# A hybrid decoder layer: the state space model on quarter-array products, its taps turned by transposes, and attention scores with the masks first

## The chip, the cores and the metric

The kernel runs on one core of a Trainium2 chip. The metric is the device time of one execution in microseconds. Before the change three runs took 1202.39, 1202.74 and 1205.45 us; the median is 1202.74 us. All durations below come from one profiled execution of the kernel before, which itself took 1202.62 us.

## The reference

One decoder layer for two groups of requests that share weights: a prompt (16 learned meta tokens and 256 positions) and 8 sample sequences with one position each. D_MODEL is 2048; the first 1024 channels of the projection drive a state space model (SSM) of 64 groups with 16 channels and one 64-dimensional complex diagonal state each, and 16 query heads on 4 key-value heads do sliding-window attention.

```python
u, q, k, v = project(rmsnorm(x))                 # one matrix product with w_in
# state space model, per group g (16 channels h, 64 states p):
x_t  = coef * (b @ u_t);  s_t = a * s_{t-1} + x_t            # complex, diagonal
y_t  = Re(c @ s_t) + d_skip * u_t
y    = gelu(y);  y = y * sigmoid(y @ w_glu + b_glu)
# attention, banded in blocks of 128, with a learned sink per head:
o    = softmax([mask + scale * q k^T | sink])[..., :-1] @ v
x    = x + [rmsnorm(y) | rmsnorm(o)] @ w_out
x    = x + ConvFFN(rmsnorm(x))                   # 2048 -> 2 * 5632 -> 2048
```

Outputs are the layer's result, new caches of keys and values, and the new SSM and convolution states.

## The kernel before

The activations are kept transposed: channels on the 128 partitions, 280 positions (266 after the norm of the SSM and attention results) along the free axis. Every large product streams its weights once: a 512 KB tile `w` comes by DMA from the sync engine (SP) into one of three buffers, ScalarE (ACT) casts it to `wh`, VectorE (DVE) subtracts that to get the low part `wl`, and TensorE (PE) does three products for each pair of tiles (`mm3`, L233 to L235). A helper records every elementwise operation of two inputs at line L72, so these are known by their tile names.

PE runs its instructions in the order in which the code is written; the order of the other engines comes from a scheduler when the kernel is built. Each engine works through its own queue in order. The stages that matter:

- Attention and the projection of `u` (104.78 to 216.91 us). Eight groups, four of kind "A" (144 keys: the meta tokens and one block) and four of kind "B" (256 keys), go through `att_group` (L831) in turn; between its steps stand the PE instructions of the projection that makes `u`. A group has three PE steps. Scores: four heads, each with one product of the identity `identb` with the mask (L840) and one of 64 rows of `qT` with `kd` (L841), all added in one tile `sps`. Then the softmax on DVE and ACT (L856, L862) leaves `P`; eight transposes make `ppt` (L870); four products with the values make `ops` (L879), its two halves of the partitions one after the other.
- The SSM stage (216.91 to 334.47 us). The sequence is cut into chunks of CH = 4 positions, so 76 columns (68 chunks and 8 samples) stand for all positions. Iteration i of eight handles 8 of the 64 groups as 4 pairs r. `ssm_load` brings `u` and fills block-padded copies of the maps (`Bb`, `C0b`, `DI`) for it; `ssm_in` transposes `Bb` into `Li`; `ssm_fir` makes the products of the first taps (`kps`, L1077) and copies them into `FIR`; `ssm_state` takes the chunk inputs (`vps`, L1095), then runs a chain of ten DVE instructions: rotate (`z`, `q`), two scans, rotate back into `S`; `ssm_out` makes the output (`yps`, L1136) from `S` with the map `Cb`, filled by `ssm_maps`, and from `U` with `FIR`.
- The same stage carries the attention half of the output projection (`oa`): blocks of 12 matmuls (`acc<-ah`), and a table OA says how many stand at three places of each iteration. It is not changed.
- The gated product with `w_glu`, the SSM half of `w_out`, and the feed-forward network (to the end).

In the loop (L1176 on) the order written for PE within iteration i is: the inputs of state i+1 (`vps`), `oa` blocks, the output of i (`yps`), `oa` blocks, the transposes of i+2 (`lps`), `oa` blocks, the taps of i+2 (`kps`).

Of the kernel before, what the change touches and what calls it, by code (L numbers as in the profile page):

```python
# [22 lines left out]
NS = 8  # L23
# [4 lines left out]
CH = 4  # L28
# [13 lines left out]
def rope_tables():  # L42
# [12 lines left out]
        "vec1": dict(lam_re=32, lam_im=32, log_dt=32, ssm_d=32),  # L55
# [10 lines left out]
def body(ctx, tc, I, O, dbg=None):  # L66
# [389 lines left out]
    def prm_maps():  # L456
# [38 lines left out]
        R0, N0 = CC[:, :, 0, 0, :], CC[:, :, 1, 0, :]  # L495
        A.copy(R0, vsl("c_re").rearrange("p (r h) -> p r h", h=16))
        A.activation(N0, vsl("c_im").rearrange("p (r h) -> p r h", h=16), AF.Copy, scale=-1.0)
        yield
        for h in range(0, 32, 8):
            r_ = slice(h, h + 8)  # L500
            pr, pi = (PW[:, k, r_, :, None].to_broadcast([128, 8, 4, 16]) for k in range(2))
            Rb, Nb = (z[:, r_, None, :].to_broadcast([128, 8, 4, 16]) for z in (R0, N0))
            mul(w1, Rb, pr)
            yield
            mul(w2, Nb, pi)
            yield
            add(CC[:, r_, 0, 1:, :], w1, w2)
            yield
            mul(w1, Nb, pr)
            yield  # L510
            mul(w2, Rb, pi)
            yield
            sub(CC[:, r_, 1, 1:, :], w1, w2)
            yield
# [83 lines left out]
    sdp = sp.tile([128, 32], F32, name="sdp")  # L598
# [14 lines left out]
    ud = dram.tile([8, 128, CH, UC], F32, name="ud")  # L613
    yd = dram.tile([8, 128, 4, SC_], F32, name="yd")
# [175 lines left out]
    CC = sp2.tile([128, 32, 2, CH + 1, 16], F32, name="CC")  # L790
# [40 lines left out]
    def att_group(nm, kv):  # L831
# [45 lines left out]
        for par in range(2):  # L877
            for bi, (c, n, vv) in enumerate(blocks):
# [153 lines left out]
    Bbs = [sw.tile([128, 4, 2 * CH, 2, 16], F32, name=f"Bb{i}", bufs=1) for i in range(2)]  # L1032
    C0s = [sw.tile([128, 4, 2, 2, 16], F32, name=f"C0b{i}", bufs=1) for i in range(2)]
    Cb = sw.tile([128, 4, 2 * CH, 2, 16], F32, name="Cb", bufs=1)
    FIRs = [sw.tile([128, 4, CH, 32], F32, name=f"FIR{i}", bufs=1) for i in range(2)]
    DIs = [sw.tile([128, 4, 32], F32, name=f"DI{i}", bufs=1) for i in range(2)]
    for t in (Bbs[0], C0s[0]):
        V.memset(t, 0.0)
    for t in (DIs[0], FIRs[0], Bbs[1], C0s[1], Cb, DIs[1], FIRs[1]):
        G.memset(t, 0.0)  # L1040
    SO4 = SO.rearrange("p c b r -> p c r b")
    Li, U2, S, d0 = {}, {}, {}, {}

    def ssm_load(i):

        r4 = slice(4 * i, 4 * i + 4)
        U2[i] = sw.tile([128, 4, UC], F32, name="U2", bufs=3)
        for j in range(CH):
            nc.sync.dma_start(U2[i][32 * j:32 * j + 32], ud[i, :, j, :].rearrange("(r q) c -> q r c", r=4))
# [4 lines left out]
        mul(DIs[i % 2][96:128], sdp[96:128, r4, None].to_broadcast([32, 4, 32]),  # L1054
            ident[96:128, None, 96:128].to_broadcast([32, 4, 32]), eng=G)
# [3 lines left out]
    def bv(i):  # L1059
        return Bbs[i % 2].rearrange("p r (c j) g h -> p r c (j g h)", c=2)  # L1060

    def ssm_in(i):
        Li[i] = sw.tile([128, 4, 2, 128], F32, name="Li")
        lps = big.tile([128, 4, 2, 128], F32, name="lps", tag="big")
        for r in range(4):
            for c in range(2):
                PE.transpose(lps[:, r, c, :], bv(i)[:, r, c], ident)  # L1067
        for h in range(2):
            A.copy(Li[i][:, 2 * h:2 * h + 2], lps[:, 2 * h:2 * h + 2])

    def ssm_fir(i):
        FIR = FIRs[i % 2]
        C0v = C0s[i % 2].rearrange("p r c g h -> p r c (g h)")
        kps = one.tile([128, 4, 32], F32, name="kps", tag="one")
        for r in range(4):
            for c in range(2):
                PE.matmul(kps[:, r, :], bv(i)[:, r, c], C0v[:, r, c], start=c == 0, stop=c == 1)  # L1077
        add(kps[96:128], kps[96:128], DIs[i % 2][96:128])
        A.copy(FIR[:, :, 3], kps)
        for j in range(3):  # L1080
            A.copy(FIR[32 * j:32 * j + 32, :, 2], kps[32 * j + 32:32 * j + 64])
        A.copy(FIR[0:64, :, 1], kps[64:128])
        A.copy(FIR[0:32, :, 0], kps[96:128])

    def ssm_state(i):
# [6 lines left out]
        vps = big.tile([128, 4, 2, 128], F32, name="vps", tag="big")  # L1092
        for r in range(4):
            for c in range(2):
                PE.matmul(vps[:, r, c, :SC_], Li[i][:, r, c, :], U2[i][:, r, NS:UC], start=True, stop=True)  # L1095
# [3 lines left out]
        def both(x):  # L1099
            return x[:, :, None].to_broadcast([128, 4, 2, SC_])  # L1100

        mul(z.rearrange("p c r n -> p r c n"), vps[:, :, :, :SC_], both(cs))
        mul(q.rearrange("p c r n -> p r c n"), vps[:, :, ::-1, :SC_], both(sn))
# [17 lines left out]
    def ssm_maps(i):  # L1121
        r4 = slice(4 * i, 4 * i + 4)
        for g in range(2):
            p = slice(64 * g, 64 * g + 64)
            A.copy(Cb[p, :, :, g, :].rearrange("p r (c j) h -> p r c j h", c=2), CC[p, r4, :, 1:, :])

    def ssm_out(i):
        Cv = Cb.rearrange("p r (c j) g h -> p r c (j g h)", c=2)
        yps = one.tile([128, 4, SC_], F32, name="yps", tag="one")
        for r in range(4):  # L1130
            for part in range(3):
                if part < 2:
                    lhs, rhs = Cv[:, r, part], S[i][:, part, r, 0:SC_]
                else:
                    lhs, rhs = FIRs[i % 2][:, r].rearrange("p j q -> p (j q)"), U2[i][:, r, 0:SC_]
                PE.matmul(yps[:, r, :], lhs, rhs, start=part == 0, stop=part == 2)  # L1136
        ysb = sw.tile([128, 4, SC_], F32, name="ysb")
        A.copy(ysb, yps)
# [9 lines left out]
    def gelu(i):  # L1148
        yr = gy.tile([128, CH, SC_], F32, name="yr", bufs=2)
        for r in range(4):  # L1150
            nc.sync.dma_start(yr[32 * r:32 * r + 32], yd[i, :, r, :].rearrange("(j q) c -> q j c", j=CH))
# [214 lines left out]
def prepare(I):  # L1366
# [9 lines left out]
    def gp(v):  # L1376
        v = v.reshape((32, 128) + v.shape[2:])
        return np.moveaxis(v, 0, 1).reshape(128, -1)

    qg, kg = I["q_norm_g"][0], I["k_norm_g"][0]  # L1380
# [3 lines left out]
    v = dict(norm_mix_g=col(I["norm_mix_g"]), norm_ffn_g=col(I["norm_ffn_g"]), ssm_out_g=col(I["ssm_out_g"]),  # L1384
             attn_out_g=col(I["attn_out_g"]), b_glu=col(I["b_glu"]),
# [5 lines left out]
             h0=np.concatenate(h0, 1), ssm_d=np.tile(I["ssm_d"][0].reshape(32, 32).T, (4, 1)),  # L1391
# [40 lines left out]
```

## Time and profile before

| what | value |
|---|---|
| median of three runs | 1202.74 us |
| profiled execution, its own time | 1202.62 us (span in the trace 1200.4 us) |
| PE busy, share of the span | 1172.8 us, 98% |
| chain that ended last: PE, DVE, ACT | 91%, 3%, 3% of the span |
| DVE busy, share of the span | 813.0 us, 68% |
| ACT busy, share of the span | 608.4 us, 51% |
| POOL (GpSimd) busy, share of the span | 97.1 us, 8% |
| mean granted clock of PE | 0.987 |

The span is the time between the first and the last instruction in the trace; some 2.2 us of the execution lie around it. A busy share is an average over stages with different limits. The rows below are of three kinds: single groups of instructions in order of time (start, busy time, engine, line, operation, output from inputs, count; in brackets idle time ahead and what ended it), stretches with the busy time of each engine, and all instructions of a tile or a line (shortest, median and longest duration in ns). A count such as "x2" beside one matmul of 32-bit data is two passes over its columns.

### The profile page before, as it was taken

How to read it: one execution, taken by the hardware profiler on the slowest of the kernel's cores; microseconds unless marked ns; L12 is line 12 of the kernel's file. 1: busy time of each engine (PE TensorE's matmuls, PEld its weight loads, DVE VectorE, ACT ScalarE, POOL GpSimd, SP SyncE). 2: the span in 40 equal slices, each digit the busy share in tenths (PEclk: the TensorE clock that was granted, in tenths of full speed). 3: DMA queues.
4: the chain of work that ended last, by engine and by line, in shares of the span. 5: the costliest groups of instructions: out<-in, count | busy, mean ns of one | idle time of the engine just before them, and what ended most of it. 6: DMA issues, size and time to landing. Idle time of an engine off the chain costs nothing.

```text
span 1200.4 us, 23033 instructions
## 1 busy us (share of the span) xinstructions
PE 1172.8 (98%) x9184; PEld 1133.7 (94%) x9184; DVE 813.0 (68%) x1469; ACT 608.4 (51%) x1009; POOL 97.1 (8%) x243
## 2 busy tenths in 40 slices
PE   7999999899998999999999999999999999999998
PEld 6887878799997999999999999999999999999998
DVE  8798767488778967676767644446767676764443
ACT  5567557566564654454445433334445444543332
POOL 1020121322014200000000000000000000000000
PEclk9999889799999999999999999999999999999999
DMA  8445344434465655555555555555555555556664
GB/s 272 142 140 169 98 129 145 135 87 118 114 184 158 193 160 178 179 179 180 178 176 176 169 181 187 180 182 178 180 181 179 178 176 176 176 187 199 201 198 128
DMA packets 237114, 201.90 MB, mean 168 GB/s; under 512 B 16152, under 2 KB 233256, under 8 KB 236968
## 3 DMA queue, kind: packets, MB, share of 16 engines
q1 hardware_dynamic: 233856, 193.88, 52.9%
q10 hardware_dynamic: 2608, 3.58, 0.9%
q0 software_dynamic: 544, 2.97, 0.7%
q8 instruction: 72, 1.18, 0.5%
q14 instruction: 34, 0.28, 0.1%
HBM read 194.59 MB, written 8.25 MB: 169 GB/s over the span
## 4 chain that ended last, share of the span: by engine, by line
PE 91%; DVE 3%; ACT 3%; issue 1%; DMA 1%; SPq 0%; POOL 0%; ACTq 0%; DVEq 0%; POOLq 0%
PE acc L233 27%; PE acc L235 26%; PE acc L234 26%; PE yps L1136 2%; PE sps L841 2%; PE kvb L571 1%; DVE wl L72 1%; PE ops L879 1%; PE kps L1077 1%; ACT wh L216 1%; PE ppt L870 1%; PE vps L1095 1%; PE sps L840 1%; PE lps L1067 0%; DMA w<-w_in 0%
## 5 line engine op out<-in xcount | busy, mean ns | idle before, releaser
L72 DVE TENSOR_TENSOR wl<-w,wh 128x1024 fp32r<-128x1024 f32 (+1 forms) x348 | 419.8, 1206 | 306.4 <-ACT wh L216 302.2
L216 ACT CAST wh<-w 128x1024 fp32r<-128x1024 f32 (+1 forms) x348 | 358.2, 1029 | 493.4 <-PE acc L234 332.4
L233 PE MATMUL acc<-x2h,wh 128*128 128x266 f32 x1408 | 397.0, 287 | 0.7 <-DVE os L72 0.7
L234 PE MATMUL acc<-x2l,wh 128*128 128x266 f32 x1408 | 395.7, 286 | 0.0
L235 PE MATMUL acc<-x2h,wl 128*128 128x266 f32 x1408 | 375.0, 287 | 0.0
L234 PEld LDWEIGHTS acc<-x2l,wh 128*128 128x128 f32 x1408 | 267.1, 190 | 0.1
L233 PEld LDWEIGHTS acc<-x2h,wh 128*128 128x128 f32 x1408 | 265.9, 189 | 0.9 <-issue 0.9
L235 PEld LDWEIGHTS acc<-x2h,wl 128*128 128x128 f32 x1408 | 254.2, 189 | 0.1
L234 PE MATMUL acc<-hl,wh 128*128 128x264 f32 x704 | 196.1, 284 | 0.0
L233 PE MATMUL acc<-hh,wh 128*128 128x264 f32 x704 | 196.0, 284 | 0.0
L235 PE MATMUL acc<-hh,wl 128*128 128x264 f32 x704 | 184.2, 284 | 0.0
L234 PEld LDWEIGHTS acc<-hl,wh 128*128 128x128 f32 x704 | 132.3, 188 | 0.0
L233 PEld LDWEIGHTS acc<-hh,wh 128*128 128x128 f32 x704 | 132.3, 188 | 0.0
L235 PEld LDWEIGHTS acc<-hh,wl 128*128 128x128 f32 x704 | 126.1, 188 | 0.0
L233 PE MATMUL acc<-xh,wh 128*128 128x266 f32 (+1 forms) x256 | 78.8, 308 | 0.0
L235 PE MATMUL acc<-xh,wl 128*128 128x266 f32 (+1 forms) x256 | 75.9, 296 | 1.7 <-DVE wl L72 1.5
L234 PE MATMUL acc<-xl,wh 128*128 128x266 f32 (+1 forms) x256 | 75.8, 296 | 0.0
L1314 POOL COPY coll<-up 128x10 f32<-128x10 f32 x88 | 16.9, 192 | 634.1 <-DVE up L72 633.9
L233 PEld LDWEIGHTS acc<-xh,wh 128*128 128x128 f32 x256 | 50.3, 196 | 4.4 <-issue 3.4
L235 PEld LDWEIGHTS acc<-xh,wl 128*128 128x128 f32 x256 | 49.9, 195 | 2.4 <-DVE wl L72 2.3
L234 PEld LDWEIGHTS acc<-xl,wh 128*128 128x128 f32 x256 | 50.2, 196 | 0.1
L1317 ACT ACTIVATE ct<-up,cin 128x256 f32<-128x256 f32 x88 | 48.1, 594 | 0.0
(371 smaller groups left out, 1579.5 us busy)
## 6 DMA issues: line engine op xcount, KB each, us to landing
w<-w_up SPq DMA_DIRECT2D x176, 512.0 KB, 3.5
w<-w_down SPq DMA_DIRECT2D x64, 512.0 KB, 3.4
w<-w_in SPq DMA_DIRECT2D x40, 512.0 KB, 3.7
w<-w_out SPq DMA_DIRECT2D x32, 512.0 KB, 3.8
w<-w_down SPq DMA_DIRECT2D x32, 384.0 KB, 3.2
w<-w_glu SPq DMA_DIRECT2D x8, 512.0 KB, 3.7
buf<-x_t SPq DMA_DIRECT2D x4, 532.0 KB, 6.8
out_y<-buf ACTq DMA_DIRECT2D x8, 264.0 KB, 4.1
```

The lines of the kernel that those rows point to most:

```text
L72: return eng.tensor_tensor(o, a, b, op=op)
L216: A.copy(wh[:, :nk, :], w[:, :nk, :])
L233: PE.matmul(ps, wh, xh, start=st, stop=False)
L234: PE.matmul(ps, wh, xl, start=False, stop=False)
L235: PE.matmul(ps, wl, xh, start=False, stop=sp)
L571: PE.matmul(kv_ps[f], kw[b][:, j, cc], xs[:, b + j, :], start=b + j == 0, stop=False)
L840: PE.matmul(sps[:, r % 2, r // 2, :nk], identb, maskb[nm][:, :nk], start=True, stop=False)
L841: PE.matmul(sps[:, r % 2, r // 2, :nk], qT[p, h // 2, q0:q0 + 128], kd[p, kv, k0:k0 + nk], start=False, stop=True)
L870: PE.transpose(ppt[:n, bi, r, :], P[:, r, c:c + n], ident)
L1136: PE.matmul(yps[:, r, :], lhs, rhs, start=part == 0, stop=part == 2)
L1314: G.tensor_copy(coll[:, n, :], up[:, NR - 10:NR])
L1317: A.activation(t, up[:, 2:258], AF.Identity, scale=cin[:, n, 2:3], bias=cin[:, n, 3:4])
```

## The change

Attention: in each group two products write the masks first, each over two heads at once, and the four score products follow in a row, on alternating halves of the partitions. The value products are reordered so that the two halves of the output partitions alternate.

State space model: `u` is stored by tap and group, and each half of the partitions loads all of it (two DMAs instead of four). The input and output maps are then used as they lie, as quarter-array products of 64 rows and 64 columns (`vps` 16 instead of 8 products, `yps` 24 instead of 12 into two tiles), so that the block-padded copies `Bb`, `Cb`, `FIR` and `DI` go, with their zero fills. The taps are made in 32-column tiles beside the transposes of `ssm_in`, one small DVE sum `kz` puts the skip term in, and `ssm_fir` makes four shifted copies of `kz` on POOL, each turned by a transpose on PE, and one ACT copy makes `FIR`. The small copies `C0b` move from ACT to POOL. The storing of `u` takes four DMAs for each of eight tiles instead of one. Rows of two weights and some vectors are permuted on the host to fit.

```diff
 def att_group(nm, kv):
+        for b in range(2):
+            PE.matmul(sps[:, b, :, :nk], identb, maskb[nm][:, None, :nk].to_broadcast([128, 2, nk]), start=True, stop=False)
         for r in range(4):
...
-            PE.matmul(sps[:, r % 2, r // 2, :nk], identb, maskb[nm][:, :nk], start=True, stop=False)
-            PE.matmul(sps[:, r % 2, r // 2, :nk], qT[p, h // 2, q0:q0 + 128], kd[p, kv, k0:k0 + nk], start=False, stop=True)
+            PE.matmul(sps[:, r % 2, r // 2, :nk], qT[p, h // 2, q0:q0 + 128], kd[p, kv, k0:k0 + nk], start=False, stop=r >= 2)
...
-        for par in range(2):
-            for bi, (c, n, vv) in enumerate(blocks):
+        for bi, (c, n, vv) in enumerate(blocks):
+            for par in range(2):
                 PE.matmul(ops[64 * par:64 * par + 64], vv[:n, 64 * kv:64 * kv + 64], pts[bi][:n, par::2, :],
...
 def u_evac(i):
-            nc.sync.dma_start(ud[i], uu)
+            for j in range(CH):
+                nc.sync.dma_start(ud[i, j].rearrange("h r c -> r h c"), uu[:, j, :])
...
 def ssm_load(i):
-            A.copy(Bbs[i % 2][q, :, :, g, :], BB[q, r4].rearrange("p r c j h -> p r (c j) h"))
-            A.copy(C0s[i % 2][q, :, :, g, :], CC[q, r4, :, 0, :])
-        mul(DIs[i % 2][96:128], ..., eng=G)
+            G.tensor_copy(C0s[i % 2][q, :, :, g, :], CZ[q, r4])
...
+    def ssm_in(i):
+        lps = lpk[i][:, 0]
         for r in range(4):
-            for c in range(2):
-                PE.transpose(lps[:, r, c, :], bv(i)[:, r, c], ident)
-        for h in range(2):
-            A.copy(Li[i][:, 2 * h:2 * h + 2], lps[:, 2 * h:2 * h + 2])
+            PE.transpose(lps[:, r, :], bmap(i, r), ident)
+        A.copy(Li[i], lps)
+        for c in range(2):
+            for r in range(4):
+                PE.matmul(ktp[32 * r:32 * r + 32]..., C0s[i % 2][:, r, c]..., bmap(i, r)[:, 64 * c:64 * c + 64], start=c == 0, stop=c == 1)
+        kz = kzs[i % 2]
+        A.copy(kz[:, 0:CH - 1], ktp[:, 0:CH - 1])
+        add(kz[:, CH - 1], ktp[:, CH - 1], eyed[:, i])
...
+    def ssm_fir(i):
+        for j in range(CH):
+            k = sw.tile([128, 2, 64], F32, name="kz2", bufs=2)
+            G.tensor_copy(k, kz[:, None, CH - 1 - j:2 * CH - 1 - j, :]....to_broadcast([128, 2, 64]))
+            PE.transpose(fps[:, j, :], k.rearrange("p o a -> p (o a)"), ident)
+        A.copy(FIR[i].rearrange("p r h j -> p j r h"), fps.rearrange("p j (r h) -> p j r h", h=16))
...
 def ssm_state(i):
-                PE.matmul(vps[:, r, c, :SC_], Li[i][:, r, c, :], U2[i][:, r, NS:UC], start=True, stop=True)
+            for g in range(2):
+                for c in range(2):
+                    x, y = slice(64 * c, 64 * c + 64), slice(64 * g, 64 * g + 64)
+                    PE.matmul(vps[y, c, r, :SC_], Li[i][x, r, y], U2[i][x, 2 * r + g, NS:UC], start=True, stop=True)
...
 def ssm_out(i):
+        for h in range(2):
+            for part in range(3):
+                for o in range(2):
+                    for g in range(2):
+                        r, x, y = 2 * h + o, slice(64 * g, 64 * g + 64), slice(64 * o, 64 * o + 64)
...
+                        PE.matmul(yps[g][y, h, :SC_], lhs.rearrange("p h j -> p (h j)"), rhs, start=part == 0, stop=part == 2)
...
-        ssm_maps(i)
```

What moves is shown at three places. First PE at the scores of the first attention group (kind A): before, mask and score alternate.

```order
549 L840 LDWEIGHTS identb
550 L840 MATMUL sps<-maskA,identb 128x144
551 L841 MATMUL sps<-buf 128x144
552 L840 LDWEIGHTS identb
553 L840 MATMUL sps<-maskA,identb 128x144
554 L841 MATMUL sps<-buf 128x144
555 L840 LDWEIGHTS identb
556 L840 MATMUL sps<-maskA,identb 128x144
557 L841 MATMUL sps<-buf 128x144
```

The same place of the changed kernel (`buf` is the tile of queries and keys):

```order
549 L841 LDWEIGHTS identb
550 L841 MATMUL sps<-maskA,identb 128x2x144
551 L841 LDWEIGHTS identb
552 L841 MATMUL sps<-maskA,identb 128x2x144
553 L845 MATMUL sps<-buf 128x144 x4
```

Two mask products of 288 columns now stand ahead of four score products in a row, of which neighbours use different halves of the partitions.

Second, DVE in the SSM loop, from the end of one state's chain to the start of the next. Before (`kps` gets the skip term from `DI`; `oas` and `buf` are the output projection's):

```order
474 L72 TENSOR_TENSOR S<-z,csT 128x8x76
475 L72 TENSOR_TENSOR q<-z,snT 128x608
476 L72 TENSOR_TENSOR S<-S,q 128x4x76 x2
477 L72 TENSOR_TENSOR oas<-acc_2863,ors 128x266
478 L72 TENSOR_TENSOR buf<-buf,oas 128x266
479 L72 TENSOR_TENSOR wl<-w,wh 128x1024
480 L72 TENSOR_TENSOR kps<-kps,DI_2511 32x128
481 L72 TENSOR_TENSOR z<-vps,csT 128x4x2x76
```

The same place of the changed kernel (`kz` of the next state gets the skip term from `eyed`):

```order
474 L72 TENSOR_TENSOR S<-z,csT 128x8x76
475 L72 TENSOR_TENSOR q<-z,snT 128x608
476 L72 TENSOR_TENSOR S<-S,q 128x4x76 x2
477 L72 TENSOR_TENSOR kz_2515<-lps,eyed 128x16
478 L72 TENSOR_TENSOR oas<-acc_2894,ors 128x266
479 L72 TENSOR_TENSOR buf<-buf,oas 128x266
480 L72 TENSOR_TENSOR wl<-w,wh 128x1024
481 L72 TENSOR_TENSOR z<-vps,csT 128x608
```

The sum that PE's next taps need stands behind the whole chain of the state in DVE's queue, in both kernels; in the changed one four POOL copies and four transposes follow it, too.

Third, POOL in one iteration of the changed kernel (`SO` is the output of the states, `d` the decay for the scans; before, `SO` is followed by `DI` alone):

```order
95 L1124 COPY SO<-S 128x2x4
96 L72 TENSOR_TENSOR SO<-S,ah_439 128x2x4x8
97 L1055 COPY C0b_2513<-CZ 64x8x16 x2
98 L1085 COPY kz_3019<-kz_2515 128x128
99 L1085 COPY kz_3022<-kz_2515 128x128
100 L1085 COPY kz_3025<-kz_2515 128x128
101 L1085 COPY kz_3028<-kz_2515 128x128
102 L1095 MEMSET S 128x8
```

The four copies that make the taps stand behind the two instructions that store the state and behind the two `C0b` copies.

## Rows read from the trace of the kernel before

**Rows 1.** Four stretches: length, busy time (instructions) of each engine, granted clock, DMA share, GB/s.
```profile
104.78:216.91 112.13, 110.49 (x716) 86.52 (x715) 81.43 (x213) 69.85 (x183) 19.94 (x40) 0.91 0.47 145
...
250.14:307.88 57.74, 57.21 (x491) 56.41 (x490) 47.00 (x75) 39.67 (x94) 11.29 (x27) 1.00 0.38 96
307.88:334.47 26.59, 25.70 (x212) 25.30 (x211) 20.82 (x39) 14.12 (x34) 0.95 (x4) 1.00 0.57 155
...
222.92:229.75 6.83, 6.18 (x27) 6.12 (x28) 2.35 (x12) 1.51 (x4) 0.82 (x2) 0.50 0.17 30
```
**Rows 2.** PE in order of time, scores of an A group, to the instruction behind.
```profile
104.78 0.24 PE L840 MATMUL sps<-maskA,identb 128*128 128x144 bf16 x1
...
107.21 0.40 PE L233 MATMUL acc<-xh,wh 128*128 128x280 f32 x1
```
**Rows 3.** PE in order of time, scores of a B group, to the instruction behind.
```profile
200.17 0.28 PE L840 MATMUL sps<-maskB,identb 128*128 128x256 bf16 x1
200.38 0.70 PE L841 MATMUL sps<-buf 64*128 64x256 f32 x2
...
203.53 0.33 PE L870 MATMUL ppt<-ident,P 128*128 128x128 f32 x1
```
**Rows 4.** PE in order of time, value products of an A group, to the instruction behind.
```profile
122.21 0.64 PE L879 MATMUL ops<-pt,vx 16*64 16x256 f32 x2
...
124.50 0.24 PE L840 MATMUL sps<-maskA,identb 128*128 128x144 bf16 x1
```
**Rows 5.** PE in order of time, first two value products of a B group.
```profile
199.15 0.66 PE L879 MATMUL ops<-pt,vA 128*64 128x256 f32 x4
```
**Rows 6.** All products of two tiles: shortest, median, longest ns, first and last start.
```profile
L952 PE MATMUL mps<-buf x32: 172/173/175, 116.1 to 116.5; 64*2 64x16 f32 x32
...
L985 PE MATMUL mop<-mT,vx x16: 194/194/215, 148.7 to 149.1; 16*64 16x4 f32 x16
```
**Rows 7.** In order of time: transposes of the first group, softmax of the seventh.
```profile
117.56 1.63 PE L870 MATMUL ppt<-ident,P 128*16 128x128 f32 x8 [0.88 <-ACT P L862]
...
201.18 1.71 ACT L862 ACTIVATE P<-P,st 128x256 f32<-128x256 f32 x4
```
**Rows 8.** ACT and PE in order of time, ahead of the first SSM iteration.
```profile
217.28 1.24 ACT L1052 COPY Bb<-BB 64x512 f32<-64x512 f32 x2
...
222.65 0.38 ACT L814 ACTIVATE osqt<-ops 128x256 f32<-128x256 f32 x1
...
223.13 0.56 PE L185 MATMUL orps<-ones,osq 128*128 128x1 f32 x2 [3.33 <-issue]
```
**Rows 9.** PE in order of time, one SSM iteration.
```profile
250.14 1.99 PE L1095 MATMUL vps<-U,Li 128*128 128x76 f32 x16
251.92 0.37 PE L233 MATMUL acc<-ah,wh 128*128 128x266 f32 x1
...
253.82 0.67 PE L1136 MATMUL yps<-S,Cb 128*128 128x76 f32 x4 [0.17 <-ACT FIR L1083]
...
256.56 1.04 PE L1067 MATMUL lps<-ident,Bb 128*128 128x128 f32 x8
```
**Rows 10.** DVE in order of time, begin and end of two states' chains.
```profile
252.16 0.79 DVE L72 TENSOR_TENSOR z<-vps,csT 128x608 f32<-128x608 f32 x1 [0.25 <-PE vps L1095]
...
258.06 0.86 DVE L72 TENSOR_TENSOR S<-S,q 128x304 f32<-128x304 f32 x2
...
264.12 0.79 DVE L72 TENSOR_TENSOR z<-vps,csT 128x608 f32<-128x608 f32 x1 [1.51 <-PE vps L1095]
...
271.86 0.86 DVE L72 TENSOR_TENSOR S<-S,q 128x304 f32<-128x304 f32 x2
```
**Rows 11.** All POOL copies of one line, 128x128 elements, in the key stage.
```profile
L680 POOL COPY kb<-kr x6: 288/852/880, 71.4 to 75.0; 128x128 f32<-128x128 f32 x6
```
**Rows 12.** POOL in order of time, behind a state's chain.
```profile
258.98 0.20 POOL L1117 COPY SO<-S 128x8 f32<-128x8 f32 x1 [0.86 <-DVE S L72]
259.14 0.32 POOL L72 TENSOR_TENSOR SO<-S,ah 128x64 f32<-128x64 f32 x1
```

More of the change, by code (lines that the diff above doesn't have):

```diff
@@ L498, in prm_maps @@
         yield
+        c1, c2 = (w.rearrange("p a b c -> p (a b c)").rearrange("p (a b c) -> p a b c", b=16, c=4) for w in (w1, w2))
         for h in range(0, 32, 8):
             r_ = slice(h, h + 8)
-            pr, pi = (PW[:, k, r_, :, None].to_broadcast([128, 8, 4, 16]) for k in range(2))
-            Rb, Nb = (z[:, r_, None, :].to_broadcast([128, 8, 4, 16]) for z in (R0, N0))
-            mul(w1, Rb, pr)
+            pr, pi = (PW[:, k, r_, None, :].to_broadcast([128, 8, 16, 4]) for k in range(2))
+            Rb, Nb = (z[:, r_, :, None].to_broadcast([128, 8, 16, 4]) for z in (R0, N0))
+            mul(c1, Rb, pr)
             yield
-            mul(w2, Nb, pi)
+            mul(c2, Nb, pi)
             yield
-            add(CC[:, r_, 0, 1:, :], w1, w2)
+            add(CC[:, r_, 0], c1, c2)
             yield
-            mul(w1, Nb, pr)
+            mul(c1, Nb, pr)
             yield
-            mul(w2, Rb, pi)
+            mul(c2, Rb, pi)
             yield
-            sub(CC[:, r_, 1, 1:, :], w1, w2)
+            sub(CC[:, r_, 1], c1, c2)
             yield
@@ L1039, in body @@
-    for t in (DIs[0], FIRs[0], Bbs[1], C0s[1], Cb, DIs[1], FIRs[1]):
+    kzs = [sw.tile([128, 2 * CH - 1, 16], F32, name=f"kz{i}", bufs=1) for i in range(2)]
+    eye = small.tile([128, 16], F32, name="eye", tag="rq_t")
+    eyed = sw.tile([128, 8, 16], F32, name="eyed", bufs=1)
+    V.tensor_reduce(eye, ident.rearrange("p (b h) -> p h b", h=16), axis=AX.X, op=OP.add)
+    mul(eyed, eye[:, None, :].to_broadcast([128, 8, 16]), sdp[:, :, None].to_broadcast([128, 8, 16]))
+    for t in (*C0s, *kzs):
@@ L1099, in both @@
         def both(x):
-            return x[:, :, None].to_broadcast([128, 4, 2, SC_])
-        mul(z.rearrange("p c r n -> p r c n"), vps[:, :, :, :SC_], both(cs))
-        mul(q.rearrange("p c r n -> p r c n"), vps[:, :, ::-1, :SC_], both(sn))
+            return x[:, None].to_broadcast([128, 2, 4, SC_])
+        mul(z, vps[:, :, :, :SC_], both(cs))
+        mul(q, vps[:, ::-1, :, :SC_], both(sn))
         yield
@@ L1119, in ssm_state, with ssm_out @@
         yield
-    def ssm_maps(i):
-        r4 = slice(4 * i, 4 * i + 4)
-        for g in range(2):
[L1124 to L1138, printed above, removed]
+    def ssm_out(i):
+        yps = [p.tile([128, 2, 256], F32, name="yps", tag=n) for p, n in ((one, "one"), (msc, "msc"))]
+        for h in range(2):
[3 more added lines that the diff above has]
+                        r, x, y = 2 * h + o, slice(64 * g, 64 * g + 64), slice(64 * o, 64 * o + 64)
+                        if part < 2:
+                            lhs, rhs = CC[x, 4 * i + r, part], S[i][x, part, r, 0:SC_]
+                        else:
+                            lhs, rhs = FIR[i][x, 2 * r + g], U2[i][x, 2 * r + g, 0:SC_]
+                        PE.matmul(yps[g][y, h, :SC_], lhs.rearrange("p h j -> p (h j)"), rhs, start=part == 0, stop=part == 2)
+        ysb = sw.tile([128, 2, 2, SC_], F32, name="ysb")
+        for g in range(2):
+            A.copy(ysb[:, g], yps[g][:, :, :SC_])
         nc.sync.dma_start(yd[i], ysb)
@@ L1149, in gelu @@
         yr = gy.tile([128, CH, SC_], F32, name="yr", bufs=2)
-        for r in range(4):
-            nc.sync.dma_start(yr[32 * r:32 * r + 32], yd[i, :, r, :].rearrange("(j q) c -> q j c", j=CH))
+        for k in range(4):
+            nc.sync.dma_start(yr[32 * k:32 * k + 32], yd[i, :, k // 2, k % 2, :].rearrange("(q j) c -> q j c", j=CH))
         yield
@@ L1378, in gp @@
         return np.moveaxis(v, 0, 1).reshape(128, -1)
+    cp = np.arange(1024).reshape(8, 2, 2, 2, 16).transpose(0, 3, 1, 2, 4).reshape(-1)
     qg, kg = I["q_norm_g"][0], I["k_norm_g"][0]
@@ L1402, in prepare @@
     a["state_conv"] = I["state_conv"][0]
[L1403 removed]
+    for n in ("w_in", "w_up", "w_down"):
         a[n] = I[n][0]
+    a["w_glu"] = np.ascontiguousarray(I["w_glu"][0][cp][:, cp])
+    a["w_out"] = np.concatenate([I["w_out"][0][cp], I["w_out"][0][1024:]])
     return a
```

66 lines of the change are left out of this document (26 added, 40 removed).

## The prediction

> **What bounds the kernel now.** I first read the stretches [rows 1]. Between 104.78 and 216.91 us (attention with the projection of u) PE is busy for 110.49 of 112.13 us, and in five SSM iterations (250.14 to 307.88) for 57.21 of 57.74, so both stages end when PE is through with its list. In the second, DVE has 47.00 us of work, not far behind. Then I followed PE in order of time at each place that the diff touches [rows 2 to 5, 9], looked up what elsewhere runs in halves or quarters of the array [rows 6], and read the softmax [rows 7], the start of the SSM stage [rows 8] and the chain of a state on DVE and POOL [rows 10 to 12]. The rest of the kernel (before 104.78, after 334.47) is not touched: I take it as unchanged.
>
> **Attention.** Where PE is the bound, what its list loses is won. A B group's scores take 203.53 - 200.17 = 3.36 us now [rows 3]. A mask of 256 columns is followed by its score after 0.21 us [rows 3]; 256 columns at 2.4 GHz are 0.107 of that, the rest is a drain between a product of 128 rows and one of 64. A score is two passes, each at two cycles a column: 2 x 0.213 us. After the change: two masks of 512 columns, 2 x 0.213; two pairs of scores, each pair at once on the two halves of the rows, 2 x 0.427; some 0.3 for one first weight load and two drains. That is 1.58, so 1.78 less. For an A group the same with 144 columns (0.24 + 0.48 + 0.3 = 1.02) against 107.21 - 104.78 = 2.43 [rows 2]: 1.41 less.
>
> Do halves run at once? 32 passes with 64 rows start between 116.1 and 116.5 us, 13 ns apart, and each is 172 ns long [rows 6], so yes for tiny passes. For 256 columns, four passes of a B group's value products on alternating column halves take 0.66 us in all, where two passes of an A group, one behind the other, take 0.64 [rows 4, 5]. So A's value products, now 124.50 - 122.21 = 2.29 us [rows 4], come to half: 1.14 less. B's run at once already: nothing won. Sum: 4 x (1.78 + 1.41 + 1.14) = 17.3 us less.
>
> What is late next is the softmax. The first group's transposes already wait 0.88 us for P [rows 7]: what its scores lose comes back, 1.4. In the seventh, P is ready at 202.89 and the transposes start at 203.53 [rows 3, 7]; the scores between lose 1.78, so 1.1 comes back. In the others P is ready well ahead. Attention: 17.3 - 2.5 = **14.7 us less**. Bounds: 6.2, if only the mask switches go (0.93 per group's scores, less waits), to 17.3.
>
> **SSM stage, start.** ACT makes block-padded copies from 217.28 on and reaches osqt only at 222.65, so PE idles 3.33 us before orps [rows 8], and then runs 6.83 us at half its clock (0.50, which is 1.2 GHz) [rows 1]. These copies go. With 8 us of PE work behind 216.91, I place the first input product at about 225. But the next ones then wait for the new loop below: two cycles of 11.75 put the third at 248.6, against 250.14 [rows 9]: 1.5 less; bounds 4 less (POOL free) to 2 more (half clock stays).
>
> **SSM stage, loop.** PE's work in an iteration shrinks. vps takes 251.92 - 250.14 = 1.78 us in 16 passes [rows 9]; as 32 quarter passes, four at once, I take 0.75 (bounds 0.5, each pass at a quarter of the present pace, and 1.9, one every 57 ns, the pace at which the column-half pairs of 16 products at 148.7 to 149.1 come [rows 6]). yps takes 256.56 - 253.82 = 2.74; 48 quarter passes 1.1 (bounds 0.7 and 2.8). lps halves to about 0.5, the taps' tiles add 0.4, four transposes 0.45. With three oa blocks at 1.7 at most (251.92 to 253.82 less 0.17 idle) that is 8.3 us of the present 57.74 / 5 = 11.55 [rows 1, 9].
>
> Yet PE can't run ahead, since the order makes a circle: the chain of state i on DVE, then kz of i+1 (behind it in DVE's queue), then on POOL the two SO instructions, two C0b copies and four kz copies, then the last transposes, which stand directly ahead of vps(i+1), then the chain of i+1. Its length: vps 0.75; chain 6.8 (252.16 to 258.92) [rows 10]; kz 0.3 with its releases; SO 0.5 [rows 12]; C0b 2 x 0.4; kz copies 2.3; last transposes 0.3. Sum 11.75. The C0b copies have half the partitions of the copies in [rows 11] and as many columns; I take nearer their shortest, 0.29, than their longest, 0.88. For the kz copies, the same form as there: 0.29 alone, 0.85 beside DVE's work; I take two of each, as DVE goes on with other work behind the chain (bounds 1.2 and 3.4). All four need only two buffers, so a copy also waits for the transpose two before it.
>
> So an iteration is 0.2 longer than now, and DVE sets it instead of PE. In two of the five chains oa's evacuations and a weight split stand inside the chain (8.6 us instead of 6.8, 264.12 to 272.7 [rows 10]): 3.6 more; the last two iterations load no C0b: 0.8 less. Five cycles: 58.75 + 3.6 - 0.8 = 61.5 against 57.74, **3.8 more**. PE's smaller work is worth nothing here.
>
> **SSM stage, tail.** Behind the last vps PE is the bound again (25.70 of 26.59 busy [rows 1]): two yps at 1.64 less and a vps at 1.03 less are 4.3, and half of the 0.9 idle goes: **4.8 less**. The SSM stage in all: -1.5 + 3.8 - 4.8 = -2.5.
>
> **Clock.** PE now idles some 3.5 us in each cycle. After its one such idle in the stage now, it ran for 6.83 us at 0.50 [rows 1, 8]. I charge 1.5 us (half of such a stretch, where PE has work that matters), between 0 and the price of the third rival.
>
> **Rest.** The output map's copies leave ACT and the zero fills leave POOL and DVE: off the path, nothing. SP gets three more stores for each of eight tiles and two loads less per iteration; PE's busy share in [rows 1] leaves no wait for its weights, so I take 0, up to 1.
>
> Sum: -14.7 - 2.5 + 1.5 = -15.7. From the profiled execution's 1202.62 that is 1186.9; the median of the runs is 0.12 above it, so **1187 us**.
>
> **Two rules.** The passes in [rows 6] start 13 ns apart. The Trainium skill (TensorE: Matmul & The Clock Gate, section "Wait — 56ns, not 53.3ns?") says that starts never come closer than about 25 ns however few the columns. This trace does not agree, so the measurement decides; by the rule vps would be at least 0.8 and yps 1.2 us, an estimate, some 0.2 more per cycle. In [rows 3] 0.1 us goes at a change between 128 and 64 rows. The skill (TensorEngine Tiling (Array Packing), Key Properties) says that such a change of mode drains TensorE, which agrees, and speaks against this change in the loop, where all products were full-size: six changes per iteration at 0.1 are 0.6 us, an estimate, beside which PE still idles; in the tail about 1 us comes back by it.
>
> **Rivals.** *POOL alone (A):* the copies run at 0.29 each because DVE's work there does not slow them: 2.3 falls to 1.2 and C0b by 0.25, 1.35 less per cycle, 6.8 in five and 1.5 at the start: 1179. For it: DVE waits in each cycle once the bound is a circle. Against: DVE has oas, buf and wl to do just then.
> *Softmax (B):* more groups wait for P than the two, as DVE and ACT serve u and the SSM maps between: only 8 of the 14.7 stay: 1194. For it: the first group's wait; against: in the other six P is ready well ahead.
> *Tiles one by one (C), slower:* parts of the array don't overlap with these lengths, passes come every 57 ns. Attention wins 6.2; vps costs 1.1 more in seven cycles and the tail, yps 1.7 more twice: 12.5 more. 1187 + 8.5 + 12.5 = 1208. Against it: [rows 4 to 6].
> *Half clock in the loop (D), slower:* PE's idle in each cycle brings it to 1.2 GHz throughout. Its 8.3 us become 16.6, more than the circle's 11.75; it decides from the point at which over 3.4 us of a cycle's work is at half clock. 4.85 x 5 at the end of the five cycles, 3 before: 1202.6 - 14.7 - 2.5 + 24.3 + 3 = 1213. For it: [rows 1, 8]. Against: in the loop PE never idles 3.3 us at a stretch, since oa blocks stand between.
> *No effect:* the masks or halves don't do what the order says; I see no way.
>
> **Numbers.** Forecast 0.57; A 0.17, B 0.12, C 0.06, D 0.08. A run of this kernel can't tell 0.3% (3.6 us) from no change, so "faster" is below 1199. All of A and B and nearly all of the forecast are below it: 0.82. Near it lies a mix of B with a part of D: 0.06. C, D: slower, 0.12 less what falls within, rounded to 0.12. The range is 1174 (A with all 17.3 of attention) to 1201 (B with a part of D), which leaves out about 0.18. The likeliest case's own range is 1182 to 1192.
>
> **What would show it.** Right: in each group four scores take under 1.1 us (A) or 1.7 (B), value products of A about 1.15; the stage up to oa's first block is 13 to 16 us shorter; vps and yps are under 0.9 and 1.3 long; PE idles 2 to 5 us in each SSM iteration until a kz copy on POOL, and iterations take 11.5 to 12.5 us. Wrong: PE busy throughout the loop (C or D, told apart by the granted clock there), iterations under 11 us (A), PE waiting for P in more than two groups (B), or any change behind 334.

## The result and the profile after

The changed kernel takes 1187.34 us (median; 1185.71 to 1187.65), against 1202.61 for the kernel before in the same comparison: ratio 0.9865, 95% interval 0.9848 to 0.9882. The forecast was 1187. The total is right to 0.4 us, but two of its terms are wrong by several microseconds each, with opposite signs, so the stages matter more than the sum. The profiled execution has a span of 1185.5 us, 14.9 less than before.

Stretches of the changed kernel, with the columns of [rows 1]: attention, the start of the SSM stage to the third vps, five iterations, the end to the first gated product.

```profile
103.79:197.36 93.57, 90.40 (x699) 75.71 (x698) 79.74 (x213) 69.29 (x183) 22.02 (x44) 0.93 0.60 174
197.36:229.27 31.91, 23.93 (x267) 19.74 (x265) 22.30 (x46) 9.62 (x18) 13.96 (x31) 0.84 0.36 101
229.27:289.49 60.22, 46.80 (x690) 39.73 (x689) 45.76 (x75) 23.48 (x48) 21.44 (x50) 0.89 0.37 103
289.49:319.49 30.00, 24.62 (x274) 22.98 (x274) 19.89 (x36) 11.76 (x27) 0.48 (x2) 0.90 0.50 139
```

Against [rows 1], with the boundaries at the same instructions:

| stage | before | after | difference | forecast |
|---|---|---|---|---|
| to the first scores | 104.78 | 103.79 | -1.0 | 0 |
| attention | 112.13 | 93.57 | -18.6 | -14.7 |
| SSM, to the third vps | 33.23 | 31.91 | -1.3 | -1.5 |
| SSM, five iterations | 57.74 | 60.22 | +2.5 | +3.8 |
| SSM, end | 26.43 | 30.00 | +3.6 | -4.8 |
| clock, charged apart | | | | +1.5 |
| rest | 866.1 | 866.0 | -0.1 | 0 |

The end is taken here to the start of the first gated product (334.31 before), [rows 1] has it 0.16 later. The first line is scatter: in the runs below the first scores start anywhere from 103.46 to 104.93 us, though the code ahead of them is the same.

PE at the scores of an A group and of a B group, and at the value products of an A group, after the change (answering to [rows 2 to 4]):

```profile
103.79 0.42 PE L841 MATMUL sps<-maskA,identb 128*128 128x288 bf16 x2
104.14 0.76 PE L845 MATMUL sps<-buf 64*128 64x144 f32 x8
104.83 0.40 PE L233 MATMUL acc<-xh,wh 128*128 128x280 f32 x1
...
121.33 0.65 PE L883 MATMUL ops<-pt,vx 16*64 16x256 f32 x4
121.91 0.65 PE L883 MATMUL ops<-pt,vA 128*64 128x256 f32 x4
122.50 0.42 PE L841 MATMUL sps<-maskA,identb 128*128 128x288 bf16 x2
...
170.77 0.60 PE L841 MATMUL sps<-maskB,identb 128*128 128x512 bf16 x2
171.31 1.13 PE L845 MATMUL sps<-buf 64*128 64x256 f32 x8
172.37 0.40 PE L233 MATMUL acc<-xh,wh 128*128 128x280 f32 x1
```

From the first row of a group to the instruction behind it: scores 1.04 us (A) and 1.60 (B), value products 1.17. The forecast had 1.02, 1.58 and 1.15.

One SSM iteration after the change: first PE without the output projection, then POOL (answering to [rows 9, 11, 12]).

```profile
229.27 0.76 PE L1102 MATMUL vps<-U,Li 64*64 64x76 f32 x32
231.63 0.49 PE L1139 MATMUL yps<-S,CC 64*64 64x76 f32 x16
...
239.76 0.56 PE L1086 MATMUL lps<-ident,kz 128*128 128x128 f32 x2 [1.47 <-POOL kz L1085]
240.51 0.56 PE L1086 MATMUL lps<-ident,kz 128*128 128x128 f32 x2 [0.18 <-POOL kz L1085]
241.00 0.76 PE L1102 MATMUL vps<-U,Li 64*64 64x76 f32 x32
```
```profile
237.14 0.20 POOL L1124 COPY SO<-S 128x8 f32<-128x8 f32 x1 [1.60 <-DVE S L72]
237.29 0.33 POOL L72 TENSOR_TENSOR SO<-S,ah 128x64 f32<-128x64 f32 x1
237.56 1.79 POOL L1055 COPY C0b<-CZ 64x128 f32<-64x128 f32 x2
239.42 0.53 POOL L1085 COPY kz<-kz 128x128 f32<-128x128 f32 x2
240.16 0.53 POOL L1085 COPY kz<-kz 128x128 f32<-128x128 f32 x2 [0.21 <-PE lps L1086]
```

The circle is there as forecast: chain, SO, C0b, copies, transposes, vps, in 11.73 us. Inside, two terms differ in this iteration: the C0b copies took 1.8 us, not 0.8, and the kz copies 0.53 a pair, not 1.15; together they came out near the forecast. Other iterations mix them otherwise. Over the five, the shortest, median and longest kz copy took 286, 296 and 1287 ns, and the iterations 11.73, 14.29, 11.77, 11.18 and 11.25 us. The longest has DVE work of the output projection (oas, buf, wl) inside its chain, as the forecast had for two of the five; the second such one, without C0b, is the one of 11.18.

The end of the stage is where the forecast failed. ScalarE's queue there, in order of time:

```profile
296.46 0.21 ACT L1157 ACTIVATE yT<-yr 128x2 f32<-128x2 f32 x1 [5.75 <-DMA yr<-yd]
...
297.24 0.45 ACT L1142 COPY ysb<-yps 128x152 f32<-128x152 f32 x2
...
303.64 0.20 ACT L1157 ACTIVATE yT<-yr 128x2 f32<-128x2 f32 x1 [4.07 <-DMA yr<-yd]
...
304.41 0.46 ACT L1142 COPY ysb<-yps 128x152 f32<-128x152 f32 x2
...
314.45 0.20 ACT L1157 ACTIVATE yT<-yr 128x2 f32<-128x2 f32 x1 [5.49 <-DMA yr<-yd]
```

An output goes from PSUM by a copy (ysb) and a store (yd) to memory, back by a load (yr) and into the gelu (yT). PE's last output products end at 298.7 us, but their copy runs at 304.41, since in ACT's queue it stands behind the gelu of the iteration before, which waits for its transfer. In the kernel before, the last ysb stood ahead of that gelu, and DVE's yl did not wait for its store:

```profile
322.07 0.41 ACT L1138 COPY ysb<-yps 128x304 f32<-128x304 f32 x1 [1.67 <-PE yps L1136]
323.97 0.20 ACT L1153 ACTIVATE yT<-yr 128x2 f32<-128x2 f32 x1 [1.48 <-DMA yr<-yd]
...
327.44 1.82 DVE L72 TENSOR_TENSOR yl<-yT,yh 128x266 fp32r<-128x266 f32 x5 [0.16 <-ACT yh L1259]
```

In the changed kernel PE waits four times in the end. The first two waits are for weight splits (wl) whose casts stand behind gelus in ACT's queue. The other two are larger and come from one DVE instruction (yl, the low part of the gelu's results) that waits until the last store has landed; DVE's oas and wl stand behind it. By the code, yl is opened behind `ssm_ctx.close()`, where the tiles of the SSM stage, ysb among them, have given up their memory; that this is the reason for its wait was not tested.

```profile
310.40 1.82 DVE L72 TENSOR_TENSOR yl<-yT,yh 128x266 fp32r<-128x266 f32 x5 [3.33 <-DMA yd<-ysb]
...
299.94 0.39 PE L235 MATMUL acc<-ah,wl 128*128 128x266 f32 x1 [0.74 <-DVE wl L72]
307.13 0.39 PE L235 MATMUL acc<-ah,wl 128*128 128x266 f32 x1 [0.75 <-DVE wl L72]
312.71 0.36 PE L233 MATMUL acc<-ah,wh 128*128 128x266 f32 x1 [2.61 <-DVE oas L72]
314.44 0.59 PE L235 MATMUL acc<-ah,wl 128*128 128x266 f32 x1 [1.25 <-DVE wl L72]
```

These four are 5.35 of the 5.38 us for which PE is idle in the end (30.00 - 24.62). For the last gelu, at 314.45, PE does not wait.

### The profile page after: what moved, and what is told of

It reads as the page before. It is cut to its first block, busy times and chain, and to the rows that moved or that the text cites. A ratio compares the mean times of both kernels' runs of the same rounds, so it can differ in the third digit from the quotient of the medians.

```text
span 1185.5 us, 23608 instructions
## 1 busy us (share of the span) xinstructions
PE 1135.8 (96%) x9488; PEld 1095.5 (92%) x9488; DVE 809.5 (68%) x1469; ACT 578.3 (49%) x929; POOL 115.0 (10%) x280
## 4 chain that ended last, share of the span: by engine, by line
PE 86%; DVE 5%; DMA 3%; ACT 2%; issue 1%; SPq 1%; POOL 1%; ACTq 0%; DVEq 0%; POOLq 0%
PE acc L233 26%; PE acc L235 26%; PE acc L234 26%; DVE wl L72 2%; DMA yd<-ysb 2%; PE kvb L572 1%; DMA yr<-yd 1%; PE ppt L874 1%; ACT wh L216 1%; PE ops L883 1%; SPq L1155 1%; PE sps L845 0%; POOL kz L1085 0%; PE osp L942 0%; DVE S L72 0%
```

## Experiments

Each was timed in five rounds beside the kernel before; the ratio is to that kernel. For comparison: the changed kernel has 0.9865 (0.9848 to 0.9882).

**The attention part alone** (the att_group lines of the diff put into the kernel before).

> The attention part of the change alone (masks first, halves alternating, value products reordered), with the state space model as before. Theory: in the trace of the changed kernel the attention stage is 18.6 us shorter (93.57 against 112.13 us), of which 14.7 is work and waits at full clock and 3.9 comes from half-clock stretches that cover 13.6 instead of 21.3 us of it. The stage owes nothing to the edits of the state space model, so this kernel takes 1184 to 1188 us. Rival: part of the stage's gain is due to the fills and copies that the other edits took from POOL and DVE; then it stays above 1190.

Measured 1184.8 us, ratio 0.9854 (0.9839 to 0.987). The attention stage takes 94.33 us, at a mean granted clock of 0.96 and with PE busy for 87.66 of it. The whole gain of the change is in this part, and the state space model's part adds nothing to it.

**The state space model's part alone** (the same lines undone in the changed kernel).

> The state space model's part of the change alone, with the attention as before. Theory: its stage from the first block of the output projection to the first gated product takes 122.1 us after the change against 117.4 before, so this part costs 4.7 us: 1206 to 1209 us. Rival (what I forecast): the part gains about 1 us, 1200 to 1203, and the loss seen in the changed kernel comes from its stage being entered in another phase of the clock.

Measured 1219.67 us, ratio 1.0147 (1.0131 to 1.0162): slower by 17, far more than either theory had. The parts don't add up: -18 and +17 alone, -15 together. One iteration took 20.75 us. Its rows on ACT, DVE and SP (SP's time is that of its queue, issue and wait together):

```profile
259.60 1.28 ACT L1156 ACT_TABLE_LOAD   x1 [9.04 <-DMA yr<-yd]
...
261.63 1.03 ACT L216 CAST wh<-w 128x1024 fp32r<-128x1024 f32 x1
...
262.69 1.22 DVE L72 TENSOR_TENSOR wl<-w,wh 128x1024 fp32r<-128x1024 f32 x1 [9.84 <-ACT wh L216]
263.83 0.78 DVE L72 TENSOR_TENSOR z<-vps,csT 128x608 f32<-128x608 f32 x1
...
232.28 17.92 SPq L209 DMA_DIRECT2D w<-w_out  x2
250.31 0.53 SPq L1051 DMA_DIRECT2D U<-ud  x1
250.89 0.58 SPq L1142 DMA_DIRECT2D yd<-ysb  x1
...
255.30 2.56 SPq L1154 DMA_DIRECT2D yr<-yd  x4
```

The first gelu's table load stands at the head of ACT's queue and waits 9.04 us for its transfer, with a weight cast behind it. DVE waits for that cast, and the next state's z stands behind DVE's wl, so every engine stops. The store adds 3.4 us to that, since it stands in SP's queue behind weight loads that wait for a buffer: its copy ended at 247.5, it was issued at 250.89. In the changed kernel the same two instructions of ACT stand the other way round, the cast first, and the same gelu's wait is 2.6 us. This order is the scheduler's choice; no edit asked for it.

**Gelus later, in that kernel.**

```diff
-        yr = gy.tile([128, CH, SC_], F32, name="yr", bufs=2)
+        yr = gy.tile([128, CH, SC_], F32, name="yr", bufs=3)
...
+        bz = {}
+        if i < 7:
+            nul = gy.tile([128, 1], F32, name="nul", bufs=2)
+            A.activation(nul, ysbs[min(i + 2, 7)][:, 1, 0, 0:1], AF.Copy, scale=0.0)
+            bz = dict(bias=nul)
-        A.activation(yT[:, i, 0:2], yr[:, 2:4, NS + 3], AF.Gelu_apprx_tanh)
+        A.activation(yT[:, i, 0:2], yr[:, 2:4, NS + 3], AF.Gelu_apprx_tanh, **bz)
...
             next(gels[i - 1])
-            next(gels[i - 1])
+        if i >= 2:
+            next(gels[i - 2])
...
+    next(gels[6])
     next(gels[7])
```

> The state space model's part alone (attention as before), with one difference on ScalarE: each gelu of the loop stands two output copies later in its queue (its zero bias is made from a later ysb; three buffers for its input instead of two). Theory: that part alone took 1219.7 us, and one of its iterations 20.75 us, since ScalarE waited 9.0 us for the first gelu's transfer with the weight cast wh behind it, so that wl, the next z on DVE and PE's products all stood still. With the gelu later no cast waits for a transfer: that iteration comes to about 12 us and the kernel to 1207 to 1212. Rival: the loss comes from the half clock (64.8 us of half clock between 95 and 345 us of that trace) and stays: above 1216.

Measured 1207.99 us, ratio 1.0053 (1.004 to 1.0066). The long iteration is 11.73 us, five take 60.2 as in the changed kernel. So 12 of the 17 us are the gelus' places in ACT's queue (the edit moves all of them), 9.0 of them this one iteration, and the rival on the clock falls.

**Copies ahead of gelus at the end of the changed kernel.**

```diff
+        if i in (5, 6):
+            nul = gy.tile([128, 1], F32, name="nul", bufs=2)
+            A.activation(nul, ysbs[i + 1][:, 1, 0, 0:1], AF.Copy, scale=0.0)
+            bz = dict(bias=nul)
...
+        A.activation(yT[:, i, 0:2], yr[:, 2:4, NS + 3], AF.Gelu_apprx_tanh, **bz)
...
```

> The changed kernel with one difference in the order of ScalarE: in the last two iterations the copies ysb of the output stand ahead of the gelu of the iteration before (a small activation of 128x1 from ysb gives the gelu its zero bias, so that it cannot run earlier). Theory: in the changed kernel the last output products end at 298.6 us, but their copy runs at 304.4, behind a gelu that waits for a transfer, and the store, the load and the last gelu follow one after the other, until 315.3; PE waits at 312.7 and 314.4. With the copy at about 299 the last gelu ends near 310, and the stage is 5 to 7 us shorter: 1180 to 1183 us. Rival: the end of the stage is set by PE's own work and its half clock; then it changes by less than 1.5 us.

Measured 1187.76 us, ratio 0.9885 (0.9868 to 0.9902): no difference. My theory of ACT's order alone fell. The copy did move ahead, and the next queue took over, as ACT and SP show:

```profile
301.21 0.46 ACT L1143 COPY ysb<-yps 128x152 f32<-128x152 f32 x2
...
304.70 1.26 SPq L1144 DMA_DIRECT2D yd<-ysb  x1
310.73 2.47 SPq L1156 DMA_DIRECT2D yr<-yd  x4
```

The store is issued 3 us after its copy ended, behind the loads of the output before and three others in SP's queue, at 304.70 where it was at 304.89, and the load that waits for it comes 6 us later. The end alone is shorter by 2.3 us (27.71 instead of 30.00), but the start of the stage is 1.6 longer (33.48), with granted clocks of 0.94 and 0.82; in the total nothing is left of it.

**Both waits of the end taken away** (gelus later as above, and the stores from ACT's queue).

```diff
-        nc.sync.dma_start(yd[i], ysb)
+        nc.scalar.dma_start(yd[i], ysb)
```

> The changed kernel with each gelu two output copies later in ScalarE's queue, and with the stores of the output (yd) issued from ScalarE's queue, right behind their copies, instead of from the sync engine's, where they stand behind weight loads that wait for a buffer. Theory: putting the copies ahead of the gelus alone changed nothing (1187.8 against 1187.3), since the last store then waited in the sync engine's queue (copy at 301.2, store at 304.7, landed near 310.7, last gelu at 315). With both gone the end of the stage is 3 to 7 us shorter; the loop's circle through DVE and POOL stays as it is, so five iterations stay at 58 to 60 us: 1180 to 1185 us. Rival: the round trip of a store and a load through memory itself sets the end: less than 2 us.

Measured 1181.16 us, ratio 0.9831 (0.9816 to 0.9845). The last store is issued at 300.34, and yl no longer waits for it. The end takes 21.66 us instead of 30.00, with PE busy for 21.27 of it, while the five iterations keep 58.53 us:

```profile
232.27:290.80 58.53, 46.05 (x690) 39.07 (x689) 46.01 (x76) 24.79 (x49) 21.76 (x50) 0.91 0.40 111
290.80:312.46 21.66, 21.27 (x274) 20.45 (x273) 19.22 (x35) 14.20 (x33) 0.48 (x2) 1.00 0.62 170
```

26.43 - 21.66 = 4.8 us less than before: what the forecast had for the end, now that PE sets it.

**The circle opened**, in three steps. First the skip term alone:

```diff
-                          bmap(i, r)[:, 64 * c:64 * c + 64], start=c == 0, stop=c == 1)
+                          bmap(i, r)[:, 64 * c:64 * c + 64], start=c == 0, stop=False)
+        PE.matmul(ktp[:, CH - 1], ident, eyed[:, i], start=False, stop=True)
...
-        A.copy(kz[:, 0:CH - 1], ktp[:, 0:CH - 1])
-        add(kz[:, CH - 1], ktp[:, CH - 1], eyed[:, i])
+        A.copy(kz[:, 0:CH], ktp)
```

> The changed kernel with only the first part of the opened circle: the skip term is added by a PE product into the taps' tile, so that no DVE instruction of the taps stands behind the state's chain; the four POOL copies still stand behind the two SO instructions (which wait for the chain) in most iterations and have two buffers. Theory: the circle is held by POOL's order as much as by DVE's, so only 0.2 to 0.5 us per iteration goes: 1184 to 1187 us. Rival: the place of the skip sum in DVE's queue alone closes the circle; then most of the opened circle's gain is here already, below 1182.

Measured 1193.17 us, ratio 0.9923 (0.9909 to 0.9938), slower than the changed kernel. One iteration took 19.72 us: in ACT's queue of this kernel, too, the first gelu stands ahead of a weight cast, and waits 8.57 us. The other iterations take 10.4 to 13.6 us, 12.3 in mean, so the skip sum's place in DVE's queue does not close the circle alone. That the gelu's place costs 8 us is seen a second time; the step itself can't be priced from this run.

Then also the copies right behind the taps, with four buffers instead of two:

```diff
...
+        kz2s[i] = []
+        for j in range(CH):
+            k = sw.tile([128, 2, 64], F32, name="kz2", bufs=4)
+            G.tensor_copy(k, kz[:, None, CH - 1 - j:2 * CH - 1 - j, :]....to_broadcast([128, 2, 64]))
+            kz2s[i].append(k)
...
-            k = sw.tile([128, 2, 64], F32, name="kz2", bufs=2)
...
+            k = kz2s[i][j]
```

> The opened circle without its last part: skip term by PE, tap copies right behind the taps with four buffers, but the two SO instructions still on POOL, where they stand ahead of the tap copies in two of the five iterations. Theory: the iterations in which SO stands ahead keep the circle (about 12 us), the others come to some 10.5; 1180 to 1184 us, between the changed kernel and the opened circle (1178.2). Rival: POOL's SO does not matter since the copies are the last anyway: within 1 us of the opened circle.

Measured 1179.23 us, ratio 0.9802 (0.9779 to 0.9824); five iterations take 54.4 us in the profiled execution, which itself took 1173.42, 5.8 less than the median.

Last, SO on DVE as well:

```diff
-        G.tensor_copy(SO[:, :, 0, r4], s[:, :, :, NS + NCH])
-        add(SO4[:, :, r4, 1:9], s[:, :, :, NS + NCH + 1:], ah0[:, :, r4, :], eng=G)
+        V.tensor_copy(SO[:, :, 0, r4], s[:, :, :, NS + NCH])
+        add(SO4[:, :, r4, 1:9], s[:, :, :, NS + NCH + 1:], ah0[:, :, r4, :])
```

> The changed kernel with the circle of its loop opened: the skip term is added by one more PE product into the taps' tile (not by DVE behind the state's chain), the four tap copies on POOL come right behind the taps with four buffers instead of two, and the two small instructions that store the state run on DVE instead of POOL. Theory: an iteration is now bound by the circle of chain, skip sum, POOL copies, transposes and input products (60.2 us for five iterations); with it open, DVE's own work (45.8 us for five) or PE's sets it: 9.2 to 10.5 us per iteration, the stage 8 to 13 us shorter, 1174 to 1180 us. Rival: another wait takes its place (the gelu on ScalarE that waits for its transfer, ahead of the FIR copy) or the clock does; then under 4 us are won.

Measured 1178.21 us, ratio 0.9795 (0.9773 to 0.9817); five iterations 53.9 us, and 4.7 us less at the start of the stage, in a profiled execution that itself took 1173.88, 4.3 less than the median. The theory holds for the circle in its total, though an iteration takes 10.8 us in mean where it had 9.2 to 10.5. The rival for SO was right: the step of the copies makes the gain, SO's engine adds nothing that can be told. Whether it is the copies' place or their two more buffers was not told apart. Among the waits that are left in this loop is ACT's for a gelu's transfer (3.8 us in the second iteration, with a cast behind it for which DVE waits).

**Scores in another order** (heads 0, 2, 1, 3: neighbours on the same half).

```diff
-        for r in range(4):
+        for r in (0, 2, 1, 3):
```

> The changed kernel with one difference in the attention: masks first as in the change, but the four scores of a group in the order of heads 0, 2, 1, 3, so that two neighbours use the same half of the partitions and only the second and third differ. Theory: halves at once are worth one score's passes for each pair, 0.43 us (B) and 0.24 (A), and of the three borders one is left where two can overlap: B groups lose some 0.4 us and A groups 0.25, the kernel 2 to 4 us: 1189 to 1192. Rival: all of the gain comes from fewer changes between 128 and 64 rows; then within 1 us of the changed kernel, 1186.5 to 1188.5.

Measured 1187.28 us, ratio 0.9868 (0.9853 to 0.9883): no difference. But the rival's reason is not shown either, since the halves still ran at once: a B group of this kernel takes 1.61 us, of which the eight passes of the scores have 1.07; that leaves room for four passes of 0.21 us, not eight, and in the trace the eight start in four pairs.

```profile
168.00 0.61 PE L841 MATMUL sps<-maskB,identb 128*128 128x512 bf16 x2
168.54 1.14 PE L845 MATMUL sps<-buf 64*128 64x256 f32 x8
169.61 0.40 PE L233 MATMUL acc<-xh,wh 128*128 128x280 f32 x1
```

What both orders share, and the kernel before lacks, is that no full-size product stands between the scores; their order among themselves does not matter over four.

**All of it**: circle opened, gelus later, stores from ACT.

> All of it together: the opened circle (1178.2 us alone), gelus two copies later, stores from ScalarE's queue. Theory: in the opened circle the remaining waits of the loop are ScalarE's for a gelu's transfer (3.4 to 3.8 us in each of four iterations) with casts and FIR copies behind them, while DVE is the bound else (about 9.5 us per iteration): five iterations 48 to 52 us instead of 53.9, the end 2 to 5 us shorter: 1169 to 1175 us. Rival: DVE's list and the start of the stage already set the loop; then above 1176.

Measured 1168.61 us, ratio 0.9723 (0.971 to 0.9736), faster than both kernels and than the attention part alone. Five iterations and the end:

```profile
225.71:277.22 51.51, 44.53 (x700) 38.35 (x699) 47.46 (x81) 24.36 (x49) 18.92 (x40) 0.93 0.47 128
277.22:300.55 23.33, 21.68 (x273) 20.49 (x273) 20.38 (x40) 14.75 (x34) 0.00 (x0) 1.00 0.57 157
```

DVE is now busy for 47.46 of 51.51 us: by busy time the loop has gone from PE's list (57.74) over the circle (60.22) to near DVE's list.

## Why the prediction was right and where it was wrong

- *Attention work: right.* The three durations shown came within 0.02 us. Stretches at half clock cover 21.3 us of the stage before and 13.6 after (0.91 and 0.93 in mean). Counted at full clock the stage is 112.13 - 21.3 / 2 = 101.5 us before and 93.57 - 13.6 / 2 = 86.8 after, 14.7 less, as forecast (its 17.3 - 2.5 is 14.8). PE's idle time in the stage grew from 1.64 to 3.17 us, 1.5 of the 2.5 that I let come back, so PE's own work shrank by some 16.2 instead of 17.3. These are estimates. The other 3.9 us are the clock: a smaller part of the stage ran at half clock, for a reason that no run shows. The forecast left the clock out of this stage, and put none of it into the range. The split is that of this trace: in att_alone less of the stage ran at half clock (0.96), but PE was idle for 6.7 us of it, and it took 94.33. So the 14.7 came out as a sum, and how much of the gain is clock and how much comes back as waits differs between runs.
- *Start and loop: right in kind and near in size.* -1.3 for -1.5, +2.5 for +3.8. In the start the parts differ more: the first vps came 9.9 us behind the stage's begin instead of 8, the two cycles behind it took 22.0 us instead of 23.5. That the circle through POOL bounds the loop is shown by the step that moves the copies and gives them more buffers (54.4 us). The prices of its parts on POOL were off in both directions, and one of the forecast's sums too: two iterations without C0b are 1.6 us less at its own 0.8 each, not 0.8, which makes +3.0.
- *End: wrong.* The step "behind the last vps PE is the bound again" failed: 30.00 us instead of 26.43 - 4.8 = 21.6, 8.4 us off. It took PE's busy share before the change for a bound that stays, and did not ask what the shorter PE list uncovers: gelus that wait for transfers, with the last output copy behind them in ACT's queue, the last store behind others in SP's, and DVE's yl, which waits for that store. Of the 8.4, PE's idle time is some 5 (5.38 in all, where the forecast left some 0.4), and the half clock some 3 (a mean of 0.90 in 30.00 us); these two are estimates. after_late shows the forecast's 4.8 once those waits are gone, at a clock of 1.00. By "off the path, nothing", the part "Rest" had written off just these queues.
- *Clock, +1.5:* the end ran at a mean of 0.90, the loop at 0.89. Since PE waits in the loop anyway, I count only the end's part, some 3 us of its 30.00 and twice the 1.5; what the half clock costs the loop no run tells apart.
- *The total:* -3.9 in attention, -1.3 in the loop, -1.0 scatter ahead of the first scores and -1.5 for the clock charged apart, against +8.4 in the end of the SSM stage and +0.2 in its start. That leaves the span 0.8 us above the forecast. The time is right by chance to that extent. The sign is not: it rests on the attention term, which held when it was timed alone.
- *The two rules.* 32 quarter passes of vps take 0.76 us in all at full clock (1.24 to 1.29 in three of the eight iterations, at half clock), and the yps of the iteration shown 1.0 (231.63 to 232.65). The 0.8 and 1.2 that the forecast had worked out go by the Trainium skill's floor for starts (TensorE: Matmul & The Clock Gate, "Wait — 56ns, not 53.3ns?"). The trace is below both, so products on different parts of the array start closer here than that floor. The changes of mode in the loop cost nothing that shows, since PE waits there.
- *Rivals.* A (POOL alone) was near on the kz copies (a median of 296 ns, but up to 1287) and wrong on the loop, as C0b took back what they won in the iteration shown. Of B, PE waited for P in one group, 1.8 us. C did not come. Of D, the loop did run at half clock in part (0.89), but its iterations stayed at the circle's length.

## What to carry to other kernels

When a stage's bound engine gets a shorter list, follow each result that leaves the stage to its use, through every in-order queue (copy, store, load, activation) and into what waits for its memory, before PE is taken as the bound of what is left. An instruction that waits for a transfer must not stand ahead of a weight cast or an output copy: here one such place cost 8 to 9 us of one iteration, and a scheduler may pick it after an edit elsewhere. Where a part of a change only pays together with the order around it, time the parts alone: half of this change cost 17 us by itself, and gains 16 on top of the other half once the queues are in order and the circle is open (1184.8 to 1168.6).

## What was not expected of the hardware

- Products on one half of the rows that stand one behind the other in the program as written still overlap with those on the other half behind them: the four scores of a B group take 1.07 us to the next instruction with neighbours on the same half (168.54 to 169.61) and 1.06 with alternating halves (171.31 to 172.37).
- POOL copies of the same form differ by more than four: the two C0b copies (64x128) took 0.64 to 1.8 us a pair, the kz copies (128x128) 0.29 to 1.29 each in the loop, and those of [rows 11] 0.29 to 0.88. What they depend on was not tested.
- A store of 152 KB and the load that waits for it take 9.6 us from the store's issue to the activation (304.89 to 314.45), not much less than a whole iteration.
